# Two products of 64x64 blocks in a triangular inverse, from a quarter of the TensorE array to the whole of it

## The chip, the cores and the metric

The kernel runs on one core of a Trainium2 chip. The metric is the device time of one execution in microseconds; the time of a version is the median of its runs. Engines are called as in the profile: PE is TensorE (PEld its weight loads), DVE is VectorE, ACT is ScalarE, POOL is GpSimd, SP issues the DMAs.

## The reference

One layer of a streaming encoder, on a prompt of 2048 tokens and a sample of 32 tokens, width 1024, all in float32. A mixer with two kinds of heads (a gated MLP over chunks of 128 positions, and a gated DeltaNet with four heads of 128) is followed by a feed-forward block of 4096. What matters here is the DeltaNet, whose recurrence is evaluated by chunks. For each chunk the reference solves a unit lower triangular system:

```python
    a = jnp.einsum('bhnid,bhnjd->bhnij', kb, k) * dec_strict
    lmat = a + jnp.eye(C, dtype=a.dtype)
    rhs = jnp.concatenate([v * beta[..., None], kb * jnp.exp(gc)[..., None]], axis=-1)
    sol = lax.linalg.triangular_solve(lmat, rhs, left_side=True, lower=True, unit_diagonal=True)
```

and then runs over the chunks in order, with a state of 128x128 for each head.

## The kernel before

The tokens go in two halves (`hf`), of 1024 and 1056. The kernel takes chunks of 128 tokens, eight in each half and the 32 sample tokens as a ninth in the second. For each half and head it builds the triangular matrices of the eight chunks, side by side in one buffer `nb` of 128 rows and 1024 columns (`delta_local`), inverts all eight together (`delta_inv`), stores the inverses to HBM, and later loads them again in the recurrence (`delta_chain`). So `delta_inv` runs eight times, once for each of four heads in each half.

`delta_inv` works from small blocks to large. Blocks of 16 are inverted on POOL, by a loop of 30 small operations. Then blocks of 16 are joined to blocks of 32, those to blocks of 64, and those to the whole 128, each time by two products on PE: the off-diagonal block of the inverse is minus the product of three blocks. In the last join the names are these. `M` is `nb` seen as eight blocks of 128x128. `TA` is rows 0 to 63 of the buffer `TZ`, eight blocks of 64x64, and holds the transposed inverse of the first diagonal block of 64; POOL clears it (`fill`, L379), ACT and DVE write its parts. The first product, `p3`, multiplies the upper right block of `M` with `TA`; DVE writes its negative into rows 64 to 127 of `TZ` (`z2`); the second product, `p4`, multiplies that with the inverse of the second diagonal block; DVE copies the result into `M`. Both products are eight calls, one for each chunk, with 64x64 stationary blocks, 64 moving columns, and a tile position that puts them on a quarter of the array (64 rows by 64 columns). `z1` is a buffer for the join before this one; it lies right behind `TZ` in the same slot.

All PE products outside of the inverse and a few small ones are on the whole array. The large ones (GEMM, line L398) split an f32 operand into two fp32r parts and take three matmuls for each product; tiles `BH` and `BL` are the parts of the activations, `wh` and `wl` those of the weights, `g` are the banks of the mixer's GEMMs and `f` those of the feed-forward block. Other banks are `B` (the inverse), `C` (the recurrence), `L` (the building of the matrices) and `M` (row sums and the MLP's mixing). Bank `B` is a ring of one, so each group of products of the inverse waits until the one before it has been read.

The order of all instructions is computed when the program is built. `Program.schedule` takes the operations with their dependencies, a modelled cost of each, and a priority (recurrence, inverse, local work, evacuation, GEMM), and simulates the engines: an engine takes the ready operation of highest priority. The instructions are then written in that order, and each engine runs its own in order. So when the inverse waits for another engine, the planner has placed GEMM matmuls on PE in between. For a group of products whose shape differs from that of the group before, it adds a charge for the change of tile:

```python
                if o.table and o.table != grid:
                    end += 195 if o.table == (P, P) else 135
                    grid = o.table
```

`table` is the shape of the stationary operand of the group's first call. The groups of `p3` and `p4` have a modelled cost of 880 ns each.

Of the kernel before, what the change touches and what calls it, by code (L numbers as in the profile page):

```python
# [11 lines left out]
ALU = mybir.AluOpType  # L12
# [4 lines left out]
P = 128  # L17
# [101 lines left out]
class View:  # L119
# [52 lines left out]
    def bc(self, shape):  # L172
        return self.step("broadcast_to", np.broadcast_to(np.uint8(0), shape), self.reg, list(shape))
# [149 lines left out]
class Kern:  # L323
# [83 lines left out]
    def tr(self, out, in_, ident):  # L407
        nc = self.nc
        self.p.op(PE, 114, lambda: nc.tensor.transpose(R(out), R(in_), R(ident)), [out], [in_, ident])
# [125 lines left out]
    def setup(self):  # L535
# [34 lines left out]
        rg("jk2", [(8, 896)], (P, 128))  # L570
        rg("ud", [(9, 288)], (P, 9, 32))
        rg("td", [(9, 576)], (P, 9, 32))
        self.TZ = self.slot(10, 0, (P, 8, 64))
        self.z1 = self.slot(10, 512, (P, 8, 32))
        self.xacc = self.slot(11, 0, (P, 512))
        rg("of", [(11, 512), (11, 768)], (P, 2, P))
# [112 lines left out]
    def consts(self):  # L689
        i = self.i  # L690
        ld = lambda v, src: self.dma(v, src, 4 * int(np.prod(v.shape)))
        bc = lambda v, n: self.dma(v, i[n].partition_broadcast(P))
        with self.p.at(GEMM):
            ld(self.wsT, i["wsT"])
            self.fill(self.wsT[64:128, :, 0:64], 0.0)
            bc(self.sgub, "sgub")
            bc(self.sgug, "sgug")
            ld(self.triu, i["triu"])
            ld(self.mask, i["mask"])
            ld(self.convw, i["convw"])  # L700
            ld(self.sconv, i["sconv"])
            ld(self.dngc, i["dngc"])
            bc(self.dtb, "dtb")
            bc(self.alog, "alog")
            for h in range(H):
                self.fill(self.S[h], 0.0)
            self.fill(self.halo, 0.0)
            self.fill(self.ab, 0.0)
            zero = self.slot(4, 0, (P, 1024))[:36]
            self.fill(zero, 0.0)  # L710
            for d in self.ud_d:
                self.dma(d.re("c a x -> (c a) x"), zero)
            self.fill(self.z0, 0.0)

    def ada_first(self, f, ps):

        ws = []
        for e in range(2):
            w = self.new("ada")
            self.dma(w, self.i["ada0"][f, :, 1024 * e : 1024 * e + 1024])  # L720
            ws.append(w)
        for e in range(2):
            self.mms([(ps[32 * s : 32 * s + 2, :256], self.cs[:, 4 * e + s, :], ws[e][:, 256 * s : 256 * s + 256],
                       dict(start=(e == 0), stop=(e == 1), tile_position=(0, 32 * s), skip_group_check=True))
                      for s in range(4)], 480)
        ar = self.arow[:, 256 * (f % 2) : 256 * (f % 2) + 256]
        self.act(ar, ps[:, :256], AF.Copy)
        for e in range(2):
            self.tr(ps[:, 256 + 128 * e : 384 + 128 * e], ar[:, 128 * e : 128 * e + 128], self.ident)
        m = self.modc[:, 0:2, f]  # L730
        for s in range(4):
            part = ps[:, 256:512].re("p (e s r) -> p e s r", e=2, s=4)[:, :, s, 0:2]
            self.tt(m, part, self.adab[:, 0:2, f] if s == 0 else m, ALU.add)
        self.ts(self.a1[:, f], m[:, 1], 1.0, ALU.add, self.nrm[:, 0, f : f + 1], ALU.mult)
# [406 lines left out]
    def delta_inv(self, hf, h, nb):  # L1141
# [5 lines left out]
        M = nb[:, :1024].re("p (c i) -> p c i", c=8)  # L1147
# [30 lines left out]
        kw = lambda *at: dict(start=True, stop=True, skip_group_check=True, tile_position=at)  # L1178
# [13 lines left out]
        if hf == 1:  # L1192
            self.tt(ud[:NS, 8, 16:32], pb[:NS, 128:144], ud[:NS, 8, 16:32], ALU.add)
        tr()
        TA, z1, z2 = self.TZ[0:64], self.z1, self.TZ
        self.fill(TA, 0.0)
        for a in range(4):
            pa = slice(32 * a, 32 * a + 32)
            self.cp(M[pa, :, pa], ud[pa, 0:8], ACT)
# [6 lines left out]
        e8 = lambda v: v.re("p (e i) -> p e i", e=8)  # L1206
# [12 lines left out]
        self.cp(TA[32:64, :, 0:32], e8(p2[32:64, 256:512]))  # L1219
        for p in range(2):  # L1220
            self.cp(M[lo[p], :, hi[p]], e8(p2[lo[p], 0:256]))
        p3 = self.bank("B")
        self.mms([(p3[64:128, 64 * e : 64 * e + 64], M[0:64, e, 64:128], TA[:, e], kw(0, 64)) for e in range(8)], 880)
        self.ts(z2[64:128], e8(p3[64:128, 0:512]), -1.0, ALU.mult)
        p4 = self.bank("B")
        self.mms([(p4[0:64, 64 * e : 64 * e + 64], z2[64:128, e], M[64:128, e, 64:128], kw(64, 0)) for e in range(8)], 880)
        self.cp(M[0:64, :, 64:128], e8(p4[0:64, 0:512]))
        d = self.us_d[h][hf]
        self.dma(d[:, :1024], nb[:, :1024])
# [616 lines left out]
```

## Time and profile before

| what | us |
|---|---|
| median of 3 runs | 2415.27 |
| fastest and slowest of them | 2406.06, 2415.52 |
| the profiled execution | 2432.54 |
| its span, first to last instruction | 2430.8 |
| PE busy in the span | 2363.7 |
| DVE, ACT, POOL busy | 1728.4, 1551.2, 757.9 |

The profile is of one execution, which was not one of the three timed runs. Times in its rows are microseconds from the start of the span. A matmul's length in a row includes its way through the array and overlaps with the next one's, so that the time that a group takes of PE is read from the starts of the groups around it, not from the lengths. An f32 product (not fp32r) appears as two matmul instructions, each with its own weight load.

### The profile page before, as it was taken

The numbers are of one execution on the slowest core, as the hardware profiler recorded it, in microseconds if no ns is written. First come the engines' busy times: TensorE is split into PE (matmuls) and PEld (weight loads), VectorE is DVE, ScalarE is ACT, GpSimd is POOL, SyncE is SP. The second block draws the span as 40 slices with busy tenths as digits, with TensorE's granted clock in tenths as the row PEclk, the third lists the DMA queues.
The fourth block names the chain that finished last, engine by engine and source line by source line (L and its number), as shares of the span: only waits on it lengthen the run. The fifth ranks groups of instructions, "written<-read, shape, count | busy, mean of one in ns | idle before, by whom it ended". The sixth has DMA issues, their size and how long they took to land.

```text
span 2430.8 us, 53532 instructions
## 1 busy us (share of the span) xinstructions
PE 2363.7 (97%) x18834; PEld 2209.3 (91%) x18834; DVE 1728.4 (71%) x3993; ACT 1551.2 (64%) x3705; POOL 757.9 (31%) x1055
## 2 busy tenths in 40 slices
PE   7999999999999999999999999999999999999998
PEld 4877778999989878999999999999999999999998
DVE  5556666556664646477777778889788878878796
ACT  4555556465655435365554688777897877877774
POOL 2134523212433223444434353323431212511111
PEclk9999999999999999999999999999999999999999
DMA  8688668455557767888766778786888878876773
GB/s 302 212 280 301 199 192 262 136 180 163 149 167 218 240 189 240 267 266 257 274 217 218 256 245 275 235 292 231 271 284 275 273 237 263 256 251 224 244 232 111
DMA packets 387238, 570.38 MB, mean 235 GB/s; under 512 B 71356, under 2 KB 201296, under 8 KB 386968
## 3 DMA queue, kind: packets, MB, share of 16 engines
q1 hardware_dynamic: 386968, 566.96, 72.5%
q8 instruction: 148, 2.42, 0.4%
q14 instruction: 122, 1.00, 0.1%
HBM read 432.44 MB, written 134.35 MB: 233 GB/s over the span
## 4 chain that ended last, share of the span: by engine, by line
PE 55%; DMA 17%; ACT 9%; DVE 9%; issue 5%; POOL 3%; SPq 1%; DVEq 0%; POOLq 0%; ACTq 0%
PE f L398 25%; PE g L398 22%; DVE s L352 5%; ACT s L337 5%; DMA s<-su_d 4%; PE C L398 3%; POOL s L352 2%; DMA s<-w_u 2%; ACT wh L337 2%; PE B L398 2%; DVE wl L352 1%; DVE s L357 1%; PE L L398 1%; SPq L390 1%; ACT wl L337 1%
## 5 line engine op out<-in xcount | busy, mean ns | idle before, releaser
L337 ACT ACTIVATE s<-s 128x260 fp32r<-128x260 f32 (+9 forms) x1379 | 601.6, 463 | 300.4 <-DVE s L357 82.0
L398 PE MATMUL f<-s,s 128*128 128x260 f32 x4068 | 541.3, 283 | 6.5 <-DVE s L352 4.9
L352 POOL TENSOR_TENSOR s<-s,s 128x260 f32<-128x260 f32 (+3 forms) x354 | 358.5, 1024 | 532.7 <-ACT s L337 400.1
L398 PE MATMUL f<-BH,wh 128*128 128x260 f32 x1796 | 511.1, 285 | 12.7 <-DVE s L352 11.1
L398 PEld LDWEIGHTS f<-s,s 128*128 128x128 f32 x4068 | 508.7, 188 | 11.0 <-DVE s L352 7.2
L398 PE MATMUL f<-BH,wl 128*128 128x260 f32 x1796 | 507.7, 283 | 1.1 <-DVE wl L352 1.1
L398 PE MATMUL f<-BL,wh 128*128 128x260 f32 x1796 | 506.4, 282 | 0.1
L352 DVE TENSOR_TENSOR s<-s,s 128x512 fp32r<-128x512 f32 (+5 forms) x721 | 412.3, 586 | 97.6 <-ACT s L337 63.4
L398 PE MATMUL g<-BH,wh 128*128 128x512 f32 (+2 forms) x1112 | 422.2, 380 | 0.0
L352 DVE TENSOR_TENSOR s<-f,s 128x260 f32<-128x260 f32 x856 | 345.0, 420 | 97.9 <-PE f L398 90.3
L398 PE MATMUL g<-BH,wl 128*128 128x512 f32 (+2 forms) x1112 | 392.9, 353 | 0.0
L398 PE MATMUL g<-BL,wh 128*128 128x512 f32 (+2 forms) x1112 | 391.6, 352 | 0.6 <-DVE BL L352 0.6
L398 PEld LDWEIGHTS f<-BH,wh 128*128 128x128 f32 x1796 | 337.7, 188 | 16.7 <-DVE s L352 8.2
L398 PEld LDWEIGHTS f<-BH,wl 128*128 128x128 f32 x1796 | 338.2, 188 | 1.9 <-DVE wl L352 1.9
L398 PEld LDWEIGHTS f<-BL,wh 128*128 128x128 f32 x1796 | 338.5, 188 | 0.3 <-DVE BL L352 0.3
L352 POOL TENSOR_TENSOR s<-s 128x260 f32<-128x260 f32 (+11 forms) x315 | 155.2, 493 | 475.7 <-DVE s L352 239.5
L337 ACT ACTIVATE wh<-s 128x512 fp32r<-128x512 f32 (+1 forms) x369 | 230.3, 630 | 78.6 <-DMA s<-w_u 28.3
L398 PEld LDWEIGHTS g<-BH,wh 128*128 128x128 f32 x1112 | 211.1, 190 | 26.6 <-issue 9.5
L398 PEld LDWEIGHTS g<-BH,wl 128*128 128x128 f32 x1112 | 210.2, 189 | 19.4
L398 PE MATMUL f<-BH,s 128*128 128x260 f32 x1016 | 225.5, 284 | 0.9 <-DVE s L352 0.8
L398 PEld LDWEIGHTS g<-BL,wh 128*128 128x128 f32 x1112 | 211.1, 190 | 15.0 <-DVE BL L352 1.1
L357 DVE SCALAR_TENSOR_TENSOR s<-s,s,s 128x512 f32<-128x512 f32 (+6 forms) x318 | 164.2, 533 | 76.0 <-ACT s L337 38.4
(119 smaller groups left out, 3537.7 us busy)
## 6 DMA issues: line engine op xcount, KB each, us to landing
s<-su_d SPq DMA_DIRECT2D x288, 256.0 KB, 3.9
s<-w_u SPq DMA_DIRECT2D x171, 256.0 KB, 4.2
s<-w_d SPq DMA_DIRECT2D x151, 256.0 KB, 4.2
s<-sd_d SPq DMA_DIRECT2D x106, 256.0 KB, 4.1
wr<-su_d SPq DMA_DIRECT2D x96, 256.0 KB, 4.4
wr<-w_b SPq DMA_DIRECT2D x42, 512.0 KB, 4.7
wr<-w_d SPq DMA_DIRECT2D x70, 256.0 KB, 4.8
s<-x_d SPq DMA_DIRECT2D x128, 130.0 KB, 3.9
```

The source lines that it names most:

```text
L337: self.p.op(ACT, c, lambda: nc.scalar.activation(out=R(out), in_=R(in_), func=func, **{k: R(v) for k, v in kw.items()}), [out, accum], [in ...
L352: self.p.op(eng, c, lambda: e.tensor_tensor(out=R(out), in0=R(a), in1=R(b), op=op), [out], [a, b])
L357: self.p.op(DVE, c, lambda: nc.vector.scalar_tensor_tensor(out=R(out), in0=R(a), scalar=R(s), in1=R(b), op0=op0, op1=op1), [out], [a, s, b])
L390: self.p.op(DMA, max(500, x), lambda: nc.sync.dma_start(out=R(out), in_=R(in_)), [out], [in_], lat=DMA_LATENCY + min(0, x - 500))
L398: nc.tensor.matmul(R(out), R(l), R(r), **kw)
```

## The change

`p3` and `p4` become products on the whole array. The stationary operand of `p3` is all 128x128 of a chunk's `M`, and its moving operand all 128 rows of a block of `TZ`, of which rows 64 to 127 are zero; rows 64 to 127 of the result are used as before. The stationary operand of `p4` is 128 rows and 128 columns of `TZ`, beginning at the chunk's block and running on into the next chunk's (for the last chunk into `z1`, hence the view `TZ1` and the clearing of `z1` at the start); rows 0 to 63 of `TZ` are cleared between the two products, and rows 0 to 63 of the result are used as before. The clearing ahead of the joins now covers all 128 rows of `TZ`.

```diff
-        self.TZ = self.slot(10, 0, (P, 8, 64))
+        self.TZ = self.slot(10, 0, (P, 512))
+        self.TZ1 = self.slot(10, 0, (P, 576))
         self.z1 = self.slot(10, 512, (P, 8, 32))
...
             self.fill(self.z0, 0.0)
+            self.fill(self.z1, 0.0)
...
-        TA, z1, z2 = self.TZ[0:64], self.z1, self.TZ
-        self.fill(TA, 0.0)
+        z1, tz = self.z1, self.TZ
+        TZ = tz.re("p (e i) -> p e i", e=8)
+        TA = TZ[0:64]
+        self.fill(tz, 0.0)
...
         p3 = self.bank("B")
-        self.mms([(p3[64:128, 64 * e : 64 * e + 64], M[0:64, e, 64:128], TA[:, e], kw(0, 64)) for e in range(8)], 880)
-        self.ts(z2[64:128], e8(p3[64:128, 0:512]), -1.0, ALU.mult)
+        self.mms([(p3[:, 64 * e : 64 * e + 64], M[:, e], TZ[:, e], dict(start=True, stop=True)) for e in range(8)], 880)
+        self.fill(TA, 0.0)
+        self.ts(TZ[64:128], e8(p3[64:128, 0:512]), -1.0, ALU.mult)
         p4 = self.bank("B")
-        self.mms([(p4[0:64, 64 * e : 64 * e + 64], z2[64:128, e], M[64:128, e, 64:128], kw(64, 0)) for e in range(8)], 880)
+        self.mms([(p4[:, 64 * e : 64 * e + 64], self.TZ1[:, 64 * e : 64 * e + 128], M[:, e, 64:128], dict(start=True, stop=True))
+                  for e in range(8)], 880)
         self.cp(M[0:64, :, 64:128], e8(p4[0:64, 0:512]))
```

The planner's cost of each product stays 880. The number of calls, of DVE and ACT operations and of DMAs stays the same; POOL gets one `fill` more in each inverse, and one at the start.

## The prediction

> **What bounds the kernel now.** I read the page first: its span and engine rows, then its shares of the chain that ended last.
>
> ```profile
> span 2430.8 us, 53532 instructions
> PE 2363.7 (97%) x18834; PEld 2209.3 (91%) x18834; DVE 1728.4 (71%) x3993; ACT 1551.2 (64%) x3705; POOL 757.9 (31%) x1055
> PE 55%; DMA 17%; ACT 9%; DVE 9%; issue 5%; POOL 3%; SPq 1%; DVEq 0%; POOLq 0%; ACTq 0%
> ```
>
> TensorE is the engine with nothing to spare, and POOL the one with most room. That is an average, so I next asked for the busy time by stretches. The eight inverses lie between 303 and 868 us, which the rows of their bank B show.
>
> ```profile
> L398 PE MATMUL B<-s,s x1936: 171/191/267, 302.9 to 867.2; 32*32 32x16 f32 x105, 32*32 32x32 f32 x64, 64*64 64x64 f32 x25
> ...
> 300.00:350.00 50.00, 49.30 (x643) 39.29 (x642) 31.44 (x75) 28.37 (x61) 14.34 (x41) 1.00 0.52 159
> ...
> 550.00:600.00 50.00, 50.00 (x319) 49.10 (x319) 33.48 (x95) 28.49 (x90) 12.18 (x39) 1.00 0.55 172
> ...
> 700.00:750.00 50.00, 46.00 (x495) 41.90 (x493) 24.50 (x98) 28.91 (x87) 6.24 (x8) 0.93 0.58 177
> ...
> 850.00:900.00 50.00, 50.00 (x469) 39.28 (x469) 27.07 (x72) 16.93 (x45) 11.56 (x10) 1.00 0.61 191
> ```
>
> The second number of each row is PE's busy time in 50 us, the last but two the granted clock. PE is full in the stretches of the inverses too, at full clock but for one; whatever waits in an inverse is covered by GEMM matmuls that the planner puts between. So in this stage the price of a change is the PE time that it takes or gives, and a longer chain of one inverse costs nothing while GEMMs are left to fill it. PE's waits between 300 and 960 us say the same; the longest ended by nothing that the profile shows (issue), and the others are short:
>
> ```profile
> PE B L398 <- issue: 3.7, 1, 3.7
> PE C L409 <- DVE s L366: 1.6, 1, 1.6
> ```
>
> Then I followed the first inverse through its end in the timeline (start, length, engine, line, output<-inputs, tile of the array, shape, count).
>
> ```profile
> 312.46 1.30 DVE L375 COPY s<-B 32x256 f32<-32x256 f32 x3 [1.38 <-PE B L398]
> ...
> 314.06 0.39 PE L398 MATMUL g<-BL,wh 128*128 128x512 f32 x1
> 314.29 0.40 PE L398 MATMUL g<-BH,wl 128*128 128x512 f32 x1
> 314.62 1.00 PEld L398 LDWEIGHTS B<-s,s 64*64 64x64 f32 x16 [0.36 <-issue]
> 314.62 1.14 PE L398 MATMUL B<-s,s 64*64 64x64 f32 x16
> ...
> 315.69 0.50 PE L398 MATMUL g<-BH,wh 128*128 128x512 f32 x1
> ...
> 315.82 0.52 POOL L379 MEMSET s<- 64x512 f32 x1 [0.34 <-PE B L398]
> 316.03 0.39 PE L398 MATMUL g<-BL,wh 128*128 128x512 f32 x1
> ...
> 316.15 0.69 DVE L366 TENSOR_SCALAR s<-B 64x512 f32<-64x512 f32 x1
> ...
> 316.95 0.40 PE L398 MATMUL g<-BH,wl 128*128 128x512 f32 x1
> ...
> 317.28 1.14 PE L398 MATMUL B<-s,s 64*64 64x64 f32 x16
> 318.35 0.50 PE L398 MATMUL g<-BH,wh 128*128 128x512 f32 x1
> ...
> 318.69 0.39 PE L398 MATMUL g<-BL,wh 128*128 128x512 f32 x1
> ```
>
> The group at 314.62 is p3, that at 317.28 is p4: eight calls each, and 16 instructions, since an f32 call is issued as two. GEMM matmuls start 0.23 us apart (314.06 to 314.29). From the GEMM matmul before p3 to the second one after it, 314.29 to 316.03, go 1.74 us, of which two GEMM steps are 0.46; so p3 takes **1.28 us** of PE. For p4 316.95 to 318.69 gives the same 1.28. Within it the sixteen run from 314.62 to 315.69, 1.07 us or 0.067 each; the other 0.21 us are pauses at the two edges: 0.10 on entering the 64*64 tile (314.62 instead of 314.52) and 0.11 on leaving (0.34 between the first two GEMM starts instead of 0.23).
>
> **The products on the whole array.** The change keeps the 64 moving columns and the 16 instructions of each product, but the stationary block grows from 64x64 to 128x128, and the tile is that of the GEMMs. Before has no f32 product of 128*128 with 64 moving columns. It has such products with 128 columns (the chain of the recurrence, C) and with one column (the row sums, M), which bound it from both sides.
>
> ```profile
> 328.88 0.40 PE L398 MATMUL g<-BH,wl 128*128 128x512 f32 x1
> ...
> 329.12 0.61 PE L398 MATMUL C<-s,s 128*128 128x128 f32 x4
> ...
> 329.48 0.49 PE L398 MATMUL g<-BH,wh 128*128 128x512 f32 x1
> ...
> 329.80 0.40 PE L398 MATMUL g<-BL,wh 128*128 128x512 f32 x1
> ```
>
> ```profile
> 1053.64 0.28 PE L398 MATMUL f<-BL,wh 128*128 128x260 f32 x1
> ...
> 1053.76 0.28 PE L398 MATMUL f<-BH,wl 128*128 128x260 f32 x1
> 1053.76 0.53 PEld L398 LDWEIGHTS M<-ones,s 128*128 128x128 f32 x4
> 1053.88 0.50 PE L398 MATMUL M<-ones,s 128*128 128x1 f32 x4
> ...
> 1054.24 0.37 PE L398 MATMUL f<-BH,wh 128*128 128x260 f32 x1
> ...
> 1054.44 0.28 PE L398 MATMUL f<-BL,wh 128*128 128x260 f32 x1
> ```
>
> By the same count, four instructions with 128 moving columns take 329.80 - 328.88 - 2 x 0.23 = 0.46 us, 0.115 each. Four with one moving column take 1054.44 - 1053.76 - 2 x 0.12 = 0.44 us, 0.110 each, the GEMM step there being 0.12. So the moving side hardly matters: loading a 128-wide stationary block sets the step, at 0.110 to 0.115 us against 0.067 for the 64-wide one. For 64 columns I take the middle, 0.1125: 16 x 0.1125 = 1.80 us for a product, and no pause at its edges, because the rows of C and M show none beyond these steps. That is 1.80 - 1.28 = **+0.52 us a product** (0.48 to 0.56). Two products in each of eight inverses (four heads, two halves) make 16 x 0.52 = **+8.3 us** (7.7 to 9.0), all on the full engine. The change saves the pauses, 16 x 0.21 = 3.4 us, and pays 16 x 16 x (0.1125 - 0.067) = 11.7 us for wider loads.
>
> The Trainium skill, "TensorE: Matmul & The Clock Gate", section "LDWEIGHTS (loading the stationary operand)", states that a weight load takes its number of columns over 1.2 GHz, whatever the contraction depth, which speaks against this change. An estimate from it is 106.7 against 53.3 ns, and with the pauses of the rows the sum would be +10.3 us; the rows' 0.110 and 0.067 agree with its direction, and the rows' sum is the one I use.
>
> **The new waits of p3.** Its stationary operand now covers all rows and columns of M, so p3 waits for all three DVE copies behind p2, where only the first, into TA, held it up. The row at 312.46 has the three in 1.30 us, so 0.87 us are added. In this inverse p3 started at 314.62, after all three ended at 313.76, so nothing moves; elsewhere the planner can put GEMM steps of 0.23 between. Behind p3 on PE queue the GEMMs. I cost it at nothing, and at up to 8 x 0.87 = 7 us if the cover were gone; with PE at 49 to 50 of 50 us it isn't.
>
> **The second clearing.** Between p3 and p4 POOL must now clear TA again, beside the DVE's negation of p3. The row at 315.82 shows what that looks like: POOL already runs a memset of this very shape there, because the clearing for the next head is released by p3. It ended at 316.34, before the negation ended at 316.84, and p4 came at 317.28. After the change p3 ends later by about half a microsecond, and memset, negation and p4 move together. The clearing for the next head, on all 128 rows, now waits for p4, since p4 reads all of TZ; a memset's cost goes by its 512 columns, so 0.52 us remains. That adds eight memsets, 8 x 0.52 = 4.2 us, to POOL, which is 31% busy, and one of z1 at the start, at most 0.52. The tightest of the slots in the trace is this one:
>
> ```profile
> 721.00 0.52 POOL L379 MEMSET s<- 64x512 f32 x1
> ...
> 721.75 1.14 PE L398 MATMUL B<-s,s 64*64 64x64 f32 x16
> ```
>
> The memset ended at 721.52, 0.23 us ahead of p4. Behind a late p4 wait the GEMMs, the chain of the recurrence and, through the DVE copy of p4, the store of the inverse. I take nothing for it, and price the loss of this cover as a rival. Less than nothing isn't to be had from a memset that is added. The DVE's and ACT's work and all DMAs keep their number and size.
>
> **The plan.** The planner books 880 ns for each product before and after, and no longer books its 135 and 195 ns for changes of tile. It will place other work around the inverses differently. I give this no mean and about 5 us either way, from the stalls of the trace that a new order can lose or repeat: the one issue wait of 3.7 us, and 700 to 750 us with 46.00 of 50.00 busy at 0.93 of the clock.
>
> **The sum.** The profiled execution took 2432.54 us (its span of 2430.8 and 1.7 around it), 0.7% above the median of the three timed runs, 2415.27. The term is PE time at full clock and the same in either, so 2440.8 for the profiled one and 2415.27 + 8.3 = **2423.6 us** for the median, 0.34% longer. I call 0.5%, 12.1 us, about what a measurement of this kernel can tell from no change; so the forecast is a small loss within it.
>
> **Rivals.** *The edges are all that counts* (not slower): a matmul with 64 moving columns keeps its step of 0.067 us on the whole array, the wider load being hidden under the matmul before. Then only the pauses go: 16 x -0.21 = -3.4 us, 2411.9. For it: the pauses are in the rows. Against it: the load of 0.110 in the one-column row, which no 64 columns can hide. The Trainium skill, "TensorEngine Tiling (Array Packing)", "Key Properties", states that a change of tiling mode drains the engine, and its "Instruction Overhead" that one moving column takes as long as 60; by these two alone the rival would hold. The trace agrees with the drain (0.21 us), and not with a step free of the stationary width.
>
> *POOL holds up p4* (slower): POOL runs in order, and it has small copies and powers that wait for other engines.
>
> ```profile
> POOL s L375 <- ACT s L337: 84.9, 34, 9.1
> ```
>
> That is 2.5 us a wait between 290 and 890 us. If such a copy stands ahead of the new clearing in four of the eight inverses, PE stands 4 x 2.5 = 10 us beside the 8.3, 2433.6. It decides the sign of a measurable loss from 3.8 us in all, 0.47 for each p4. For it: the slack of 0.23 at 721, and a planner whose POOL times are guesses. Against it: in the two inverses quoted the memset in this place met no such wait, and p4 is planned behind the clearing.
>
> *Loads and matmuls don't overlap* when both are short: 0.110 plus half of 0.115 is 0.1675, 16 of them 2.68 us, +1.40 a product, +22.4 us, 2437.7. Against it: the C row, where 128 columns and a 128-wide load fit in 0.115.
>
> *The change does nothing to see* would need the two terms, 11.7 and 3.4 us, to be equal; no row allows it, but a plan that loses one of the stalls above would hide the rest, about 2416.
>
> **How the numbers follow.** Forecast 0.58; POOL holding up p4 0.18; the edges alone 0.10; a better plan hiding the loss 0.08; no overlap 0.06. The range takes the forecast's 7.7 to 9.0 with the 5 us of the plan and reaches to the edges' 2411.9 and to POOL's 2433.6 with a few microseconds of the spread of the runs: 2408 to 2436. Slower by over 0.5% (above 2427.3) are nearly all of the POOL and no-overlap cases and a fifth of the forecast's, 0.34; faster (below 2403.2) only where the edges' or the better plan's case meets more good luck, 0.06; within, 0.60.
>
> **What would show it.** In the profile after: B groups of 128*128 with 64 columns, x16, spanning about 1.8 us from the GEMM start to the next instead of 1.07; no 64*64 left; the second GEMM start after them at 0.3 as after C; sixteen memsets of 512 columns, in pairs around p4, with p4 not waiting for POOL; PE's busy share unchanged. Wrong would be: groups of 1.1 us (the edges), groups of 2.7 (no overlap), or waits of PE's B for POOL over 0.5 us.

## The result and the profile after

The change made the kernel slightly slower: 2423.43 us (median of 7 runs, 2421.01 to 2426.65) against 2415.52 us for the kernel before (now the median of 7 runs, the three of the table among them). The ratio is 1.0038, with a 95% interval from 1.0023 to 1.0053. The forecast was 2423.6, 1.0034.

In the page of the profile after, these lines answer to those shown of before: the span, the engines' busy time and the shares of the chain that ended last.

```profile
span 2421.6 us, 53561 instructions
PE 2365.0 (98%) x18834; PEld 2218.3 (92%) x18834; DVE 1723.1 (71%) x3993; ACT 1550.2 (64%) x3704; POOL 761.1 (31%) x1064
PE 60%; DMA 14%; DVE 10%; ACT 8%; issue 4%; POOL 3%; SPq 1%; DVEq 0%; POOLq 0%; ACTq 0%
```

This execution's span is shorter than that of the profiled execution of before (2430.8), though the timed medians stand the other way round: the seven timed runs of before alone spread over 12.6 us, 2406.06 to 2418.70, so spans of two profiles can't be subtracted. What can be compared is a short stretch with the same instructions in it. Here is the end of the first inverse after the change, in the timeline:

```profile
311.36 0.39 PE L398 MATMUL g<-BL,wh 128*128 128x512 f32 x1
...
311.59 0.40 PE L398 MATMUL g<-BH,wl 128*128 128x512 f32 x1
311.59 1.98 PEld L398 LDWEIGHTS B<-s,s 128*128 128x128 f32 x16
311.82 1.89 PE L398 MATMUL B<-s,s 128*128 128x64 f32 x16
...
313.52 0.48 PE L398 MATMUL g<-BH,wh 128*128 128x512 f32 x1
313.75 0.69 DVE L366 TENSOR_SCALAR s<-B 64x512 f32<-64x512 f32 x1 [0.34 <-PE B L398]
313.78 0.52 POOL L379 MEMSET s<- 64x512 f32 x1 [1.78 <-PE B L398]
313.84 0.39 PE L398 MATMUL g<-BL,wh 128*128 128x512 f32 x1
...
316.15 0.40 PE L398 MATMUL g<-BH,wl 128*128 128x512 f32 x1
316.39 1.89 PE L398 MATMUL B<-s,s 128*128 128x64 f32 x16
318.09 0.48 PE L398 MATMUL g<-BH,wh 128*128 128x512 f32 x1
...
318.41 0.39 PE L398 MATMUL g<-BL,wh 128*128 128x512 f32 x1
```

Counted as in the prediction, p3 takes 313.84 - 311.59 - 2 x 0.23 = **1.79 us** of PE and p4 318.41 - 316.15 - 0.46 = 1.80, where before both took 1.28. The entry has no pause any more: p3 starts 0.23 after the GEMM matmul before it, and its first weight load, at 311.59, starts beside that matmul, where before the first load started only with p3 itself (both 314.62). Sixteen instructions go from 311.82 to 313.52, 1.70 us, 0.106 each, and 0.09 us are left at the exit. POOL's second clearing starts 0.03 us after DVE's negation, ends at 314.30, before the negation does at 314.44, and p4 comes two microseconds later. PE's waits between 300 and 960 us are short ones, and POOL is not among those it waited for:

```profile
PE L L398 <- ACT s L337: 1.6, 2, 1.1
PE C L398 <- DVE s L357: 1.6, 2, 0.8
PE C L409 <- DVE s L366: 0.9, 1, 0.9
PE C L398 <- ACT s L337: 0.8, 3, 0.3
PE B L398 <- DVE s L383: 0.4, 1, 0.4
```

### The profile page after: what moved, and what is told of

The parts are those of the page before. It is cut to its first block, busy times and chain, and to the rows that moved or that the text cites. A ratio compares the mean times of both kernels' runs of the same rounds, so it can differ in the third digit from the quotient of the medians.

```text
span 2421.6 us, 53561 instructions
## 1 busy us (share of the span) xinstructions
PE 2365.0 (98%) x18834; PEld 2218.3 (92%) x18834; DVE 1723.1 (71%) x3993; ACT 1550.2 (64%) x3704; POOL 761.1 (31%) x1064
## 4 chain that ended last, share of the span: by engine, by line
PE 60%; DMA 14%; DVE 10%; ACT 8%; issue 4%; POOL 3%; SPq 1%; DVEq 0%; POOLq 0%; ACTq 0%
PE f L398 30%; PE g L398 22%; DVE s L352 5%; ACT s L337 4%; PE C L398 3%; PE B L398 2%; DMA s<-su_d 2%; POOL s L352 2%; DVE s L357 2%; ACT wh L337 2%; DVE wl L352 2%; DMA s<-w_u 2%; PE L L398 1%; DMA wr<-w_b 1%; DMA wr<-su_d 1%
## 5 line engine op out<-in xcount | busy, mean ns | idle before, releaser
L357 DVE SCALAR_TENSOR_TENSOR s<-s,s,s 128x400 f32<-128x400 f32 (+6 forms) x318 | 164.2, 531 | 75.3 <-ACT s L337 40.4
```

Source lines behind the costliest of these rows:

```text
L357: self.p.op(DVE, c, lambda: nc.vector.scalar_tensor_tensor(out=R(out), in0=R(a), scalar=R(s), in1=R(b), op0=op0, op1=op1), [out], [a, s, b])
```

## The experiments

The experiments ran on three chips, each beside the kernel before on the same chip; ratios are to it, with 95% intervals. The medians of before differ from chip to chip (2421.6, 2425.2 and 2418.1 us), so microseconds are compared only on one chip. "The theory" is that of the prediction.

**Rows without columns.** The theory says that the columns of the stationary block set the price; the rivals blame the added rows, the clearing, or the waits. This is the kernel after the change with 64 columns in each stationary block:

```diff
-        self.mms([(p3[:, 64 * e : 64 * e + 64], M[:, e], TZ[:, e], dict(start=True, stop=True)) for e in range(8)], 880)
+        self.mms([(p3[64:128, 64 * e : 64 * e + 64], M[:, e, 64:128], TZ[:, e], kw(0, 64)) for e in range(8)], 880)
...
-        self.mms([(p4[:, 64 * e : 64 * e + 64], self.TZ1[:, 64 * e : 64 * e + 128], M[:, e, 64:128], dict(start=True, stop=True))
+        self.mms([(p4[0:64, 64 * e : 64 * e + 64], TZ[:, e], M[:, e, 64:128], kw(0, 0))
```

> The change with stationary blocks of 128 rows by 64 columns: both products keep the added zero rows, the added clearing, and the wait of p3 for all three copies, but each loads 64 columns as before. The theory (the columns of the load set the step): sixteen instructions of a product in 1.07 us by their starts and 1.28 us with the pauses, and the time of before, 2415.5 us, within 3 us. Rival 1 (the rows, the added clearing or the new waits cost it): about 2423.4 us, as after the change. Rival 2 (a tile of 128*64 has no pauses at its edges): 3.4 us below before, 2412.1.

Measured: 2418.13 us against 2421.59, ratio 0.9986 (0.9971 to 1.0000). The first p3 in its timeline:

```profile
314.25 0.40 PE L398 MATMUL g<-BH,wl 128*128 128x512 f32 x1
314.57 1.15 PE L398 MATMUL B<-s,s 128*64 128x64 f32 x16
315.65 0.50 PE L398 MATMUL g<-BH,wh 128*128 128x512 f32 x1
315.99 0.39 PE L398 MATMUL g<-BL,wh 128*128 128x512 f32 x1
```

315.99 - 314.25 - 0.46 = 1.28 us: twice the rows cost nothing. The pauses are there (0.09 us in, 0.11 out), so the second rival is wrong by its own mechanism, although the total came out 3.5 us below before, near its number. The clearing and the waits of p3 are in this kernel too, and it isn't slower: the first rival falls.

**The plan alone.** The kernel before, where `mms` gets `table=(P, P)` for p3 and p4, so that the planner books no change of tile.

```diff
-... kw(0, 64)) for e in range(8)], 880)
+... kw(0, 64)) for e in range(8)], 880, (P, P))
-... kw(64, 0)) for e in range(8)], 880)
+... kw(64, 0)) for e in range(8)], 880, (P, P))
```

> The kernel before, with the planner told that p3 and p4 are on the whole array, so that it books no change of tile for them; the instructions are those of before. The theory: PE has the same work, so 2415.5 us, within the 5 us put on the plan. The rival (the loss comes from the new order that the planner makes): 2423.4 us.

Measured: 2414.90 us against 2421.59, 0.9974 (0.9960 to 0.9988). The order that the planner makes without those charges is faster by some 6 us, not slower. The rival, a loss by the order, is out; the 5 us put on the plan were a little small.

**Products twice, on the whole array and in the quarter.** Two kernels, after and before, each with this in both products:

```diff
- for e in range(8)], 880)
+ for _ in range(2) for e in range(8)], 1760)
```

> The kernel after the change with each of the 16 products issued twice (32 instructions in place of 16, same results, the planner's cost doubled). The theory (all of a product's PE time ends up in the total): 16 x 1.80 = +28.8 us on 2423.4, 2452.2. The rival (part of it falls into time in which PE waits anyway): clearly less, down to the 14 us that half of it would give, 2437.

> The kernel before with each of the 16 products issued twice, in the 64*64 tile. The theory: sixteen more instructions of 0.067 us at no further pause, 1.07 us a product, 17.1 us above before; doubling on the whole array cost 28.8 by the rows, so the difference of the two doublings is 11.7 us, the price of the wider loads without the pauses. The rival (the products' cost lies in waits around them, not in their instructions): both doublings cost the same.

Measured on different chips: after doubled 2454.19 us, 1.0137 of before (1.0113 to 1.0162), about 33 us above it; before doubled 2435.01 us, 1.0036 (1.0018 to 1.0054), about 9 us above it by the ratio. The first p3 of each, after first:

```profile
313.24 0.40 PE L398 MATMUL g<-BH,wl 128*128 128x512 f32 x1
313.47 3.68 PE L398 MATMUL B<-s,s 128*128 128x64 f32 x32
316.96 0.48 PE L398 MATMUL g<-BH,wh 128*128 128x512 f32 x1
317.27 0.39 PE L398 MATMUL g<-BL,wh 128*128 128x512 f32 x1
```

```profile
316.50 0.40 PE L398 MATMUL g<-BH,wl 128*128 128x512 f32 x1
316.83 2.08 PE L398 MATMUL B<-s,s 64*64 64x64 f32 x32
318.83 0.50 PE L398 MATMUL g<-BH,wh 128*128 128x512 f32 x1
319.17 0.39 PE L398 MATMUL g<-BL,wh 128*128 128x512 f32 x1
```

A doubled product takes 317.27 - 313.24 - 0.46 = 3.57 us on the whole array, 1.78 more than a single one, and 319.17 - 316.50 - 0.46 = 2.21 in the quarter, 0.93 more than 1.28. For before doubled I had expected 1.07 more: sixteen further instructions go 0.058 us apart, not 0.067, and the rest of a single group's 1.28, 0.35 us, is the price of its edges. On the whole array the further ones go 0.111 apart, and 1.79 - 1.78 leaves 0.01 for the edges. The single starts in the traces of before and after say the same: in the middle of a group they lie 0.058 and 0.112 us apart. The total of after doubled, 33 us above before, is 25 to 30 above after, which lies 3 to 8 above before in its three comparisons; that fits the theory's 28.8 and not the rival's 14. The total of before doubled, +9, misses the +17 expected and also the 16 x 0.93 = 15 of its own trace. Both doubled kernels have orders of their own, as their modelled cost is doubled. The doublings differ widely, so that the cost lies in the instructions; their totals don't give its size to a few microseconds.

**The true cost in the plan.** After, with 1800 ns in place of 880 for each product.

> The kernel after the change with the planner's cost of each product set to 1800 ns in place of 880. The theory: PE's work is the same, 2423.4 us, within 5 us for another order. The rival (the low cost lets other engines be ordered too early, and PE stands for them): some of the 8 us comes back, 2419 or less.

Measured: 2423.78 us against 2421.59, 1.0017 (1.0004 to 1.0031). The theory's own 1.0034 lies outside this interval, but with the 5 us that it allows an order it begins at 1.0012; the rival's 2419 or less is 1.0014 or less. The interval holds part of both. Undecided.

**The same order, 64 columns.** To take the order out of the comparison, the 64-column version of the first experiment with the planner told `(P, P)`, the shape that it books after the change. The diff is against that version. Every engine's instructions then stand in the order of after; only the 256 matmuls of p3 and p4 differ. It ran beside after, on two chips.

```diff
-... kw(0, 64)) for e in range(8)], 880)
+... kw(0, 64)) for e in range(8)], 880, (P, P))
-... kw(0, 0))
-                  for e in range(8)], 880)
+... kw(0, 0))
+                  for e in range(8)], 880, (P, P))
```

> The kernel after the change, unaltered, so that it stands beside the others of this call on one chip. The theory: 0.3 to 0.4% above before, 8.3 us above the 64-column version with the same order.

> The kernel after the change with 64 stationary columns in p3 and p4 (128 rows as there) and the planner told that they are on the whole array. The order of every engine's instructions is then that of after the change, and only the 256 instructions of the products differ. The theory (wider loads minus the pauses is the whole loss): 16 x 0.52 = 8.3 us below after the change, which would be near before or a few microseconds below it, as far as the new order itself gains. The rival (the order carries part of the loss): less than 5 us below after.

> The kernel after the change once more, as the partner of the next run on another chip. The theory: 8.3 us above the 64-column version with the same order. The rival (the first comparison's 5.2 us is the true one, part of the wider loads falls into time that PE loses anyway): 4 to 6 us above it.

> The version with 64 stationary columns and the order of after the change, once more. The theory: 8.3 us below after; the rival: 4 to 6 us below. Products of 1.27 us in its trace under either.

| | after | 64 columns, same order | after / before | 64 columns / before |
|---|---|---|---|---|
| second chip | 2428.11 | 2422.93 | 1.0008 (0.9991 to 1.0025) | 0.9988 (0.9970 to 1.0006) |
| third chip | 2421.96 | 2415.06 | 1.0017 (1.0004 to 1.0029) | 0.9987 (0.9973 to 1.0000) |

After itself was expected 0.3 to 0.4% above before and came out at 0.08 and 0.17%: a miss. The wide block costs 5.2 and 6.9 us by the medians. By the means of twelve runs each it is 5.6 +- 3.0 and 8.0 +- 3.0, together 6.8 +- 2.1 us (95%), which holds the theory's 8.3 and also the upper part of the rival's 4 to 6. The traces of the pair on the third chip show the cause in the same place. After, then 64 columns:

```profile
312.11 0.40 PE L398 MATMUL g<-BH,wl 128*128 128x512 f32 x1
312.34 1.89 PE L398 MATMUL B<-s,s 128*128 128x64 f32 x16
314.05 0.48 PE L398 MATMUL g<-BH,wh 128*128 128x512 f32 x1
314.36 0.39 PE L398 MATMUL g<-BL,wh 128*128 128x512 f32 x1
```

```profile
313.23 0.40 PE L398 MATMUL g<-BH,wl 128*128 128x512 f32 x1
313.56 1.15 PE L398 MATMUL B<-s,s 128*64 128x64 f32 x16
314.63 0.50 PE L398 MATMUL g<-BH,wh 128*128 128x512 f32 x1
314.97 0.39 PE L398 MATMUL g<-BL,wh 128*128 128x512 f32 x1
```

1.79 against 1.28 us. PE's instructions stand in the same order in the two traces, so all sixteen products can be compared like this, each from the matmul before it to the second one after: the differences are 0.51 to 0.53 us in thirteen and 0.61 to 0.71 in three, 8.7 us together. From the matmul before the first product to the second after the last go 558.5 us against 550.9, so 7.6 of them are left over the whole stretch. The pair on the second chip gives 10.1 and 10.3, with 1.3 of it in one product of after at a low clock (0.75 between 810 and 820 us). One execution of each is not a mean, but both are near the theory's 8.3 and above the rival's 4 to 6. The comparison with before says the rest: with the price of the columns taken away, the new order and everything else in the change is about 3 us faster than before, by intervals that just reach no difference.

**Two column tiles.** If a load of 64 columns sets the step, two of them in different columns of the array might go side by side. Before, with odd chunks in the other column tile, and DVE moving their results to the right rows, two operations of 256 columns for one of 512 (not shown here):

```diff
-... (p3[64:128, 64*e : 64*e+64], M[0:64, e, 64:128], TA[:, e], kw(0, 64))
+... (p3[64*(e%2) : 64*(e%2)+64, 64*e : 64*e+64], M[0:64, e, 64:128], TA[:, e], kw(0, 64*(e%2)))
-... (p4[0:64, 64*e : 64*e+64], z2[64:128, e], M[64:128, e, 64:128], kw(64, 0))
+... (p4[64*(e%2) : 64*(e%2)+64, 64*e : 64*e+64], z2[64:128, e], M[64:128, e, 64:128], kw(64, 64*(e%2)))
```

> The kernel before with the eight calls of p3 and of p4 shared out alternately over two column tiles of the same 64 rows, so that a call can load and run beside its neighbour; half of the results land in the other 64 rows and DVE moves them, with two operations of 256 columns in place of one of 512. The theory by the 32*32 groups of the trace, where calls in four row tiles go 0.016 us apart, a quarter of the 64*64 step: half of 1.07 us and the 0.21 of pauses, 0.75 us a product, 16 x -0.53 = -8.5 us on before. The rival (column tiles of the same rows share one path for their loads and don't overlap): no change on PE, 1.28 a product, and the time of before.

> The version of before with two column tiles, once more. Its products took 0.81 us of PE in its trace (three starts: 312.64, 313.91, less two GEMM steps of 0.23), so 16 x (0.81 - 1.28) = -7.5 us on before; the first comparison gave 0.9957 of before, about -10 us, the rest being the order. The rival (that gain was the order's alone): within 3 us of before.

Measured: 2417.38 us against 2425.15, 0.9957 (0.9938 to 0.9976), and on the other chip 2410.80 against 2418.07, 0.9967 (0.9953 to 0.9982). The timeline:

```profile
312.64 0.40 PE L398 MATMUL g<-BH,wl 128*128 128x512 f32 x1
312.96 0.68 PE L398 MATMUL B<-s,s 64*64 64x64 f32 x16
313.58 0.50 PE L398 MATMUL g<-BH,wh 128*128 128x512 f32 x1
313.91 0.39 PE L398 MATMUL g<-BL,wh 128*128 128x512 f32 x1
...
315.49 0.68 PE L398 MATMUL B<-s,s 64*64 64x64 f32 x16 [0.26 <-DVE s L366]
```

Sixteen instructions in 0.62 us, 0.039 each in place of 0.067; with the pauses 313.91 - 312.64 - 0.46 = 0.81 us a product. 16 x (0.81 - 1.28) = -7.5 us, of which PE gives some back: it stands ahead of three of the sixteen products, 1.3 us in all, and for p4 of this inverse 0.26 us, until DVE has moved the results of p3. 7 to 10 us were measured. The rival, no overlap, is out by the group's length. The second chip shows that the gain repeats. It can't show that the gain is not the order's, since the order was the same there, and the plan alone was worth 6 us; two column tiles and one were not run in the same order, so how much of the 7 to 10 us the products give is not shown. That version is faster than both kernels. With the planner told `(P, P)` as well:

> Two column tiles, and the planner told that both products are on the whole array, as in the run that changed the plan alone and came out at 0.9974 of before, 6 us. If that gain is the plan's own and adds up: -7.5 - 6 = -13.5 us on before. If a new order only draws another sample of the same spread: -7.5 us within 5.

Measured: 2408.11 us against 2418.07, 0.9956 (0.9940 to 0.9972), 2.7 us below the version without that (2410.80), on the same chip. The interval goes from 7 to 14.5 us, so it holds 7.5 within 5 as well as 13.5: whether the plan's 6 us add up is undecided. With 0.9956 and 0.9957 the two orders of two column tiles have the lowest ratios of all kernels run.

## Why the prediction was right, point by point

**The products** were the term that mattered, and its size came out: +0.52 us predicted, +0.51 measured (1.79 against 1.28), in the same place of the same order. The predicted step of 0.1125 with no pause at the edges is what the runs show on the whole array: 0.111 a further instruction in the doubled group, and 0.01 us for the edges. (1.70 us between the starts, 0.106 each, is a little less because the first load ran beside the GEMM matmul before; the 0.09 at the exit makes it up.) On the side of before the 1.28 was read rightly and divided wrongly. The step there is 0.058 and not 0.067, and the edges cost 0.35 us and not 0.21. So the change saves 16 x (0.35 - 0.01) = 5.4 us where the prediction has 3.4, and pays 16 x (1.78 - 0.93) = 13.6 where it has 11.7. The two errors cancel, as both parts come from the same 1.28. The Trainium skill, "TensorE: Matmul & The Clock Gate", "LDWEIGHTS (loading the stationary operand)", states columns over 1.2 GHz for a load; an estimate from it is 106.7 ns for 128 columns and 53.3 for 64, and the traces come within 4 and 9% of that (0.111 and 0.058). That rows don't count, as the same section says, is borne out by the version with 128 rows and 64 columns (1.28 us).

**The sum** of +8.3 us is borne out only within the noise, and the exactness of 2423.6 is partly luck. The three comparisons of after with before gave +7.9, +3.0 and +3.9 us by the medians. With the order held fixed the columns cost 6.8 +- 2.1, and 8.7 by the traces of one pair; the rest of the change gave about 3 back. So the term was right, and what the sum lacked was a mean of about -3 us for **the plan**, which stood at zero with 5 us either way. The one run with only the plan changed shows that such an order can be worth 6 us. Why the new orders are faster is not settled. One stall differs in the traces: in the profiled execution of before PE stood for 3.75 us inside a group of the inverse, for nothing that the profile shows, and some microseconds behind it the GEMM matmuls of 400 columns start 0.33 us apart, where ahead of it they start 0.18 apart (granted clock 0.78 between 700 and 710 us).

```profile
703.00 0.69 PE L398 MATMUL B<-s,s 32*32 32x16 f32 x61
707.43 0.30 PE L398 MATMUL B<-s,s 32*32 32x16 f32 x5 [3.75 <-issue]
```

None of the five traces with after's order (three of after, two of the 64-column version) has such a stall. But the plan-only kernel has one of 2.51 us at the same group and the version with rows alone one of 3.40, and neither is slower than before, so this isn't the whole cause.

**The new waits of p3** cost nothing, as forecast: the 64-column versions have them and aren't slower than before.

**The second clearing** cost nothing either, but not as told. I had memset, negation and p4 move together by half a microsecond. In fact p4 moved away from p3: between them stand twelve GEMM matmuls where there were six, and in the trace after the change every one of the eight clearings ended 1.1 us or more before its p4, against 0.23 in the tightest slot before. So the rival of POOL holding up p4 did not come about, in any inverse.

**The edges alone** and **no overlap** were both excluded by the group's length: 1.70 us between starts, neither 1.1 nor 2.7.

## What to carry to other kernels

On a full TensorE, count a small product by the columns of its stationary block and by the pauses at its edges, both read from the starts of the neighbours: filling up with zeros to avoid a change of tile saved 0.34 us a product here and paid 0.85. To tell the step of a group from its edges, make the group longer: one length alone gave the right sum and the wrong parts. Where a small block sets the step, put its neighbours into other column tiles, so that the loads go side by side. And when the order of a whole program is computed from modelled costs, any edit of those costs shifts the time by a few microseconds of its own: compare versions with the same order before a loss of 0.3% is given to an instruction.

## What the runs showed of the hardware

Two 64x64 tiles in the same 64 rows do overlap, loads included. In the first p3 of that version the loads and the matmuls start in pairs, 0.007 us apart in a pair and 0.058 from pair to pair, where one tile has one start every 0.058. The group shrinks only from 1.07 to 0.62 us, since its first and last steps stay as long. The Trainium skill, "TensorEngine Tiling (Array Packing)", "Key Properties", states that different tiles can load and multiply in parallel, and the trace agrees.

Edges were dear for the two narrow tiles, whatever their rows: a product of 128*64 took 1.28 us like one of 64*64, 0.35 of it beyond sixteen steps of 0.058, and one of 128*128 took 0.01 beyond its steps. At the entry the traces show how: the first load of a narrow group starts with the group, that of a 128*128 group 0.23 us ahead of it, beside the GEMM matmul.
